# Decode's convolution rows on another DMA queue, and single instructions held at their traced place, in a two-layer Conformer and RWKV-7 step

## The chip, the core and the metric

The kernel runs on one core of a Trainium2 chip, in one launch. The metric is the device time of one execution in microseconds (us), the lower the better. The engines are named as the profile names them: PE (TensorE matmuls) with its weight loads PEld, DVE (VectorE), ACT (ScalarE), POOL (GpSimd) and SP (SyncE, which here only issues DMAs). Every engine works off its own list of instructions in order, and waits where an instruction needs a result that is not there yet.

## What is computed

One inference step of a decoder of two layers in float32, for a prompt of 1,024 rows (16 learned rows are put ahead of it) and for 8 decode rows. Layer 0 mixes tokens by a causal convolution module, layer 1 by RWKV-7 time mixing. Each is followed by a squared-ReLU MLP.

```python
D_MODEL, SEQ, DEC_BATCH, N_META, CONV_WIDTH, D_FF = 1024, 1024, 8, 16, 31, 4096

# layer 0
u = h @ w_pw1 + b_pw1
u = u[..., :D_MODEL] * sigmoid(u[..., D_MODEL:])
full = concatenate([buf, u], axis=1)                 # buf: the last 30 rows of u, state_conv
c = depthwise_conv(full, w_dw, width=31) + b_dw
out = silu(layernorm(c)) @ w_pw2 + b_pw2             # new state: full[:, -30:]

# layer 1
xx = prev - h                                        # prev: h of the row before
r, k, v = (h + xx * x_mix[i]) @ w_r, ... @ w_k, ... @ w_v
decay = exp(-exp(-softplus(-(w0 + tanh(xw @ w1) @ w2)) - 0.5))
a, g = sigmoid(a0 + (xa @ a1) @ a2), sigmoid(xg @ g1) @ g2
S = S * w + (S @ -kk) (kk * a)^T + v k^T             # for every row, 16 heads of 64
y = S @ r
out = ((groupnorm(y) + bonus) * g) @ w_o

# both
h = h + out
h = h + square(relu(rmsnorm(h) @ w_in)) @ w_out
```

One of the outputs, conv_sample, is the convolution state of the 8 decode rows: for each, 29 of its old 30 rows moved up by one and a new row behind them. The 29 old rows are copied from DRAM to DRAM by a DMA and touch no engine's memory.

## The kernel before, in words

**Work and tiles.** The 1,040 prompt rows and the 8 decode rows stand as columns, the 1,024 features as 8 blocks of 128 partitions. A float32 product is made of three matmuls: a weight block is split into hi (a cast on ACT, `L156`) and lo (a subtraction on POOL in four quarters, `L161`), an activation likewise (`L139` on ACT, `L140` on DVE), and PE adds hi by hi, hi by lo and lo by hi (`L186` to `L188`).

**Layer 0** goes over three groups of columns (352, 348, 348). At the start, group 0 is loaded (`xt0_*`) and transposed, its first weight blocks `pg0_*` and `pa0_*` are loaded and split, and PE makes `ps_g0_*` and `ps_a0_*`; the input of group 1 (`xt1_*`) is loaded and transposed into `tx1_*` in between. The convolution runs on DVE, the second product and the MLP follow. The start function (around `L690`) issues the eight copies of conv_sample on POOL's own DMA queue (`L696`), and there POOL's and ACT's instructions keep the order of the program.

**Layer 1** makes its mixer in four groups g of 272, 256, 256 and 264 columns: `prepare(g)` loads `hx` (`L863`), makes the differences `xx` (`L867`; blocks k = 2 and 5 on POOL, the other six on DVE) and the mixed inputs `mx{g}_{i}_{k}` (`L874`); PE makes `pk`, `pr`, `pv` of each pair of heads (`L900`). Each chunk c of 64 rows also needs the inverse of small triangular blocks: `inverses` loads `ni{c}` (`L1184`), runs a chain of some 60 short DVE instructions (`L1192`, `L1193`), stores it, and `front` loads it again as `p32` (`L1220`), transposes it into `x32` on DVE (`L1223`) and uses it on PE as `gg` (`L1280`). `norm_gate` normalises the result (`ey`, `eq`, `ems`, `L1452` to `L1459`), adds `ebv` (`L1476`), multiplies by the gate `egt` (`L1477`) and stores `d_z`.

**The output product.** `mixer_out(g)` runs for three column groups (328, 352, 352). It loads the residual `h1_g` (`L1572`), the gated result `zr` (`L1580`) and the weight blocks `wo{g}_{m}` (`L145`), splits `zr` into `z_h` and `z_l`, makes `ps_oo{g}_{m}` and adds it to `h1_g` on DVE (`L1590`); ACT squares the sum into `sq{g}_{m}` (`L248`). Then comes the MLP of layer 1.

**What sets the order.** A list scheduler of the framework sees the whole program and orders each engine's instructions by its own estimate of when their inputs are there. Inside `tc.manual_schedule(engines=...)` the named engines keep the order of the program. `tc.keep_in_program_order(x)` does so for one instruction: it may not go ahead of the instruction that was written before it on the same engine; others can still move.

Of the kernel before, what the change touches and what calls it, by code (L numbers as in the profile page):

```python
# [8 lines left out]
F32 = mybir.dt.float32  # L9
# [7 lines left out]
P = 128  # L17
# [29 lines left out]
def hybrid_step(tc, x_prompt, x_sample, state_conv, state_shift, state_wkv, meta_tokens,  # L47
# [10 lines left out]
    with ctx:  # L58
# [72 lines left out]
        def open_weights(stack, raw_bufs, bufs, tag):  # L131
# [3 lines left out]
            cur["bufs"] = bufs  # L135

        def split(hi, lo, src, eng_lo):

            nc.scalar.copy(hi, src)  # L139
            eng_lo.tensor_sub(lo, src, hi.bitcast(F32))  # L140
# [6 lines left out]

        def load_w(src, shape, name, eng_lo, tag="w", raw=None):

            a, b = shape  # L150
            if raw is None:
                raw = load_raw(src, shape, name)
            nb = cur["bufs"][tag]
            hi = cur["wsp"].tile([P, 8 * P], F32R, name=f"{name}_hi", tag=tag + "h", bufs=nb)
            lo = cur["wsp"].tile([P, 8 * P], F32R, name=f"{name}_lo", tag=tag + "l", bufs=nb)
            nc.scalar.copy(hi[:, :a * b], raw[:, :a * b])  # L156

            step = 2 * P if eng_lo is nc.gpsimd else a * b
            for c in range(0, a * b, step):
                cs = slice(c, min(c + step, a * b))  # L160
                eng_lo.tensor_sub(lo[:, cs], raw[:, cs], hi[:, cs].bitcast(F32))  # L161
            v = lambda t: t[:, :a * b].rearrange("p (a b) -> p a b", a=a)
            return v(hi), v(lo)

        def col_src(w, m):

            return w[:, m * P:(m + 1) * P].rearrange("(k p) c -> p k c", p=P)

        def load_col(w, m, name, eng_lo, tag="w"):
            return load_w(col_src(w, m), (KT, P), name, eng_lo, tag)  # L170

# [216 lines left out]
        with ExitStack() as l0:  # L388
# [158 lines left out]
            def conv_dec(c, c_col):  # L547
# [5 lines left out]
                for m in range(KT):  # L553
# [6 lines left out]
                    nc.gpsimd.tensor_copy(win[:, :, CB:CW], udec[:, m, :].unsqueeze(2))  # L560
                    nc.vector.tensor_mul(win, win, wdw[:, m:m + 1, :].broadcast_to([P, DEC, CW]))
                    rd = decp.tile([P, DEC], F32, name=f"rd{m}", tag="rd")
                    nc.vector.tensor_reduce(rd, win, axis=AX.X, op=ALU.add)
# [118 lines left out]
            with ExitStack() as s:  # L682
# [8 lines left out]
                first = pw1_weights(0, 0)  # L691

                def between():
                    ready.append(next(first))
                    for q in range(DEC):
                        nc.gpsimd.dma_start(o_conv_sample[0, q, 0:CB - 1, :], state_conv[0, q, 1:CB, :])  # L696
                with tc.manual_schedule(engines={nc.scalar.engine, nc.gpsimd.engine}):
                    for _ in transpose_x(0, *acts[0], between):
                        pass
                    ready.append(next(first))  # L700
# [151 lines left out]
        def prepare(g):  # L852
# [13 lines left out]
            for k in range(KT):  # L866
                (nc.gpsimd if k % 3 == 2 else nc.vector).tensor_sub(xx[:, k, :npr], hx[:, k, 0:npr], hx[:, k, 1:1 + npr])  # L867
                yield
# [66 lines left out]
        def mixer_in(g, tick):  # L935
# [86 lines left out]
            def finish(p, rk, ab, vv):  # L1022
                def trace():
# [20 lines left out]

                    n32 = pr.tile([P, 5, 32], F32, name=nm("n32", p), tag="n32", bufs=2)
                    if g == 0:
# [131 lines left out]
        def inverses(c, n):  # L1178
# [5 lines left out]
            nc.sync.dma_start(ni, blocks(d_n))  # L1184
            yield 5
            top = META if c == 0 else 32
            aside = bank(f"tt{c}", "x")[:B] if c + n == NCH else None
            for j in range(top - 2, 0, -1):
                wd = top - 1 - j
                o = aside if aside is not None else wk.tile([P, 256], F32, name=f"tt{c}_{j}", tag="tt")[:B]  # L1190
                o = o[:, :j * wd].rearrange("p (s t) -> p s t", t=wd)
                nc.vector.tensor_mul(o, ni[:, :j, j:j + 1].broadcast_to([B, j, wd]), ni[:, j:j + 1, j + 1:top].broadcast_to([B, j, wd]))  # L1192
                nc.vector.tensor_add(ni[:, :j, j + 1:top], ni[:, :j, j + 1:top], o)  # L1193
                if j % 4 == 0:
                    yield 1.5
# [13 lines left out]
        def front(c):  # L1209
# [12 lines left out]
            x32 = w_([P, KT, 32], "x32", c)  # L1222
            nc.vector.transpose(flat(x32), flat(p32))  # L1223
            mask = lambda x: m_ar[:, x].unsqueeze(1).broadcast_to([P, 4, HS])
# [216 lines left out]
        def norm_gate():  # L1441
# [20 lines left out]
            def load_rest(hf, lo, n):  # L1462

                two = [w_([P, KH * P], tag, f"{lo}_{hf}") for tag in ("ebv", "egt")]
                for t, src in zip(two, (d_bv, d_g)):
# [3 lines left out]
            def gated(pt, hf, lo, n, bv, gt):  # L1469
# [5 lines left out]
                w = KH * n  # L1475
                nc.vector.tensor_add(bv[:, :w], z[:, :w], bv[:, :w])  # L1476
                nc.vector.tensor_mul(gt[:, :w], bv[:, :w], gt[:, :w])  # L1477
# [80 lines left out]
        with ExitStack() as l1:  # L1558
# [10 lines left out]
            def mixer_out(g, residp, actp, fill, add):  # L1569
                lo, n = G2[g]  # L1570
                h1 = hl[g] = residp.tile([P, KT, cur["wide"]], F32, name=f"h1_{g}", tag="h")
                nc.sync.dma_start(h1[:, :, :n], d_h[:, :, lo:lo + n])  # L1572
                block = lambda m: load_col(rwkv_w_o[0], m, f"wo{g}_{m}", nc.gpsimd)
                z = new_acts(actp, f"z{g}", cur["wide"])
# [100 lines left out]
            add, sums = sums_of(1)  # L1675
            mixer_out(1, residp2, actp, lambda: None, add)
            g1 = group(1, actp, hidp, sums)
            fill, rest = filler(2 * KT + MLP2_POINTS, ([ranked(FN, final(0))], FB))
            add, sums = sums_of(2)
            mixer_out(2, residp2, actp2, fill, add)  # L1680
            end = []
# [41 lines left out]
```

## Time and profile before

| what | before |
|---|---|
| time, median of 3 runs (lowest, highest) | 2708.15 us (2705.03, 2711.84) |
| the profiled execution | 2712.1 us |
| its span, first to last instruction | 2710.4 us |
| granted TensorE clock, mean over the span | 0.982 |
| PE busy | 2618.3 us, 97% |
| DVE busy | 1724.8 us, 64% |
| POOL busy | 1450.1 us, 54% |
| ACT busy | 1138.6 us, 42% |
| HBM traffic over the span | 147 GB/s |

In the profile's timelines a row gives the start in us, the busy time, the engine (SPq, POOLq and ACTq are those engines' DMA issues), line and operation, the tiles without their numbers, the form, and in brackets how long the engine had idled before it and what released it. In the tables by stretch of time, each engine has its busy us and in parentheses its instructions; then come the granted clock of PE (1.00 is full), the busy share of the 16 DMA engines and GB/s.

### The profile page before, as it was taken

What the parts mean: (1) busy time and instruction counts of PE and PEld (TensorE: products, weight loads), DVE (VectorE), ACT (ScalarE), POOL (GpSimd) and SP (SyncE); (2) the same over time, 40 slices, a digit from 0 to 9 for tenths busy, and PEclk for the clock granted to TensorE, in tenths of its full rate; (3) what the DMA queues carried; (4) which work ended last, traced back from release to release, by engine and by line L of the source; (5) the groups of instructions that cost most, each with busy time, mean ns of one, the idle gap of its engine ahead of it and who ended that gap; (6) DMA issues with size and microseconds to landing.
All of it is one profiled execution on the core that took longest, in us unless ns stands there. A gap on an engine that the chain in (4) does not pass through costs nothing.

```text
span 2710.4 us, 51412 instructions
## 1 busy us (share of the span) xinstructions
PE 2618.3 (97%) x19796; PEld 2462.4 (91%) x19796; DVE 1724.8 (64%) x3584; ACT 1138.6 (42%) x2101; POOL 1450.1 (54%) x2068
## 2 busy tenths in 40 slices
PE   8999999999999999998999998979999899999998
PEld 7999999999999999777787886769999899999998
DVE  5999999997445345345767576676679643334435
ACT  5546435444444333333344544544444542222223
POOL 6677878877878775022111112366678753333331
PEclk9999999999999999999999998989999899999999
DMA  6653544554456442668768867786655632222211
GB/s 184 170 165 113 163 139 125 157 179 133 139 157 195 135 138 86 203 190 207 196 167 208 197 168 188 186 202 166 155 162 176 199 110 75 70 71 67 66 55 43
DMA packets 602058, 400.20 MB, mean 148 GB/s; under 512 B 96128, under 2 KB 548928, under 8 KB 601814
## 3 DMA queue, kind: packets, MB, share of 16 engines
q1 hardware_dynamic: 539716, 350.74, 46.4%
q10 hardware_dynamic: 53122, 18.88, 3.3%
q0 software_dynamic: 8976, 27.30, 3.1%
q8 instruction: 156, 2.56, 0.4%
q14 instruction: 88, 0.72, 0.1%
HBM read 338.94 MB, written 58.83 MB: 147 GB/s over the span
## 4 chain that ended last, share of the span: by engine, by line
PE 80%; DVE 10%; DMA 4%; issue 2%; ACT 2%; POOL 2%; ACTq 0%; SPq 0%; DVEq 0%; POOLq 0%
PE ps_in L186 8%; PE ps_in L187 8%; PE ps_in L188 8%; PE out L186 8%; PE out L187 8%; PE out L188 8%; PE pk L900 4%; PE pr L900 3%; PE pv L900 3%; PE ps_o L186 1%; PE ps_o L188 1%; PE ps_o L187 1%; PE ps_a L187 1%; PE ps_a L188 1%; PE ps_g L186 1%
## 5 line engine op out<-in xcount | busy, mean ns | idle before, releaser
L161 POOL TENSOR_TENSOR wo_lo<-wo_raw,wo_hi 128x256 fp32r<-128x256 f32 x736 | 540.2, 766 | 293.8 <-ACT wo_hi L156 289.8
L161 POOL TENSOR_TENSOR wi_lo<-wi_raw,wi_hi 128x256 fp32r<-128x256 f32 x640 | 471.3, 768 | 258.8 <-ACT wi_hi L156 250.2
L186 PE MATMUL out<-hh,wo_hi 128*128 128x352 f32 (+2 forms) x1536 | 500.0, 326 | 14.3 <-DVE hl L140 7.7
L188 PE MATMUL ps_in<-m_l,wi_hi 128*128 128x352 f32 (+2 forms) x1536 | 493.6, 321 | 3.6 <-DVE m_l L284 3.6
L353 DVE TENSOR_TENSOR h<-h,out 128x352 f32<-128x352 f32 (+2 forms) x768 | 387.4, 513 | 172.2 <-PE out L188 170.7
L186 PE MATMUL ps_in<-m_h,wi_hi 128*128 128x352 f32 (+2 forms) x1536 | 494.9, 322 | 0.7 <-ACT m_h L283 0.7
L187 PE MATMUL out<-hh,wo_lo 128*128 128x352 f32 (+2 forms) x1536 | 494.7, 322 | 0.0
L188 PE MATMUL out<-hl,wo_hi 128*128 128x352 f32 (+2 forms) x1536 | 493.5, 322 | 0.0
L187 PE MATMUL ps_in<-m_h,wi_lo 128*128 128x352 f32 (+2 forms) x1536 | 492.7, 321 | 0.0
L534 DVE SCALAR_TENSOR_TENSOR cv<-u,wdw,cv 128x352 f32<-128x352 f32 (+2 forms) x720 | 379.3, 578 | 0.6
L156 ACT CAST wi_hi<-wi_raw 128x1024 fp32r<-128x1024 f32 x160 | 167.9, 1049 | 410.5 <-PE out L188 197.7
L156 ACT CAST wo_hi<-wo_raw 128x1024 fp32r<-128x1024 f32 x184 | 192.9, 1048 | 346.0 <-PE out L188 163.6
L186 PEld LDWEIGHTS out<-hh,wo_hi 128*128 128x128 f32 x1536 | 291.3, 190 | 19.9 <-DVE hl L140 9.2
L188 PEld LDWEIGHTS ps_in<-m_l,wi_hi 128*128 128x128 f32 x1536 | 289.0, 188 | 5.7 <-DVE m_l L284 4.6
L186 PEld LDWEIGHTS ps_in<-m_h,wi_hi 128*128 128x128 f32 x1536 | 289.8, 189 | 2.9 <-ACT m_h L283 1.2
L187 PEld LDWEIGHTS out<-hh,wo_lo 128*128 128x128 f32 x1536 | 290.9, 189 | 0.8
L188 PEld LDWEIGHTS out<-hl,wo_hi 128*128 128x128 f32 x1536 | 290.0, 189 | 0.0
L187 PEld LDWEIGHTS ps_in<-m_h,wi_lo 128*128 128x128 f32 x1536 | 289.1, 188 | 0.9
L341 DVE SCALAR_TENSOR_TENSOR ps_in<-ps_in,rs_m 128x352 f32<-128x352 f32 (+2 forms) x192 | 100.5, 525 | 247.0 <-PE ps_in L188 246.6
L140 DVE TENSOR_TENSOR hl<-ps_in,hh 128x352 fp32r<-128x352 f32 (+2 forms) x192 | 98.8, 516 | 125.4 <-ACT hh L139 125.1
L342 ACT ACTIVATE ps_in<-ps_in 128x352 f32<-128x352 f32 (+2 forms) x192 | 84.9, 443 | 121.3 <-DVE ps_in L341 121.0
L900 PE MATMUL pv<-mx,wv_raw 128*128 128x256 f32 (+2 forms) x512 | 131.3, 401 | 1.2 <-ACT rk L1080 1.2
(368 smaller groups left out, 4687.9 us busy)
## 6 DMA issues: line engine op xcount, KB each, us to landing
wi_raw<-in_w_mlp_in_dram SPq DMA_DIRECT2D x160, 512.0 KB, 4.1
wo_raw<-in_w_mlp_out_dram SPq DMA_DIRECT2D x160, 512.0 KB, 3.7
wk_raw<-in_rwkv_w_k_dram SPq DMA_DIRECT2D x32, 512.0 KB, 8.3
wr_raw<-in_rwkv_w_r_dram SPq DMA_DIRECT2D x32, 512.0 KB, 5.8
wv_raw<-in_rwkv_w_v_dram SPq DMA_DIRECT2D x32, 512.0 KB
d_ab<-ab POOLq DMA_DIRECT2D x32, 512.0 KB, 4.7
pg_raw<-in_conv_w_pw_dram SPq DMA_DIRECT2D x24, 512.0 KB, 12.8
pa_raw<-in_conv_w_pw_dram SPq DMA_DIRECT2D x24, 512.0 KB, 4.1
```

The source lines that it names most:

```text
L140: eng_lo.tensor_sub(lo, src, hi.bitcast(F32))
L156: nc.scalar.copy(hi[:, :a * b], raw[:, :a * b])
L161: eng_lo.tensor_sub(lo[:, cs], raw[:, cs], hi[:, cs].bitcast(F32))
L186: nc.tensor.matmul(ps, w[0], act[0], start=first, stop=False)
L187: nc.tensor.matmul(ps, w[1], act[0], start=False, stop=False)
L188: nc.tensor.matmul(ps, w[0], act[1], start=False, stop=last)
L341: nc.vector.scalar_tensor_tensor(s, s, 0.0, rs()[:, :n], op0=ALU.max, op1=ALU.mult)
L342: nc.scalar.activation(s, s, AF.Square)
L353: nc.vector.tensor_add(hv[:, 4 * i + m, :], hv[:, 4 * i + m, :], ps[:, :n])
L534: nc.vector.scalar_tensor_tensor(acc[m][:, :n], ug[:, m, j:j + n], wdw[:, m, j:j + 1], acc[m][:, :n], op0=ALU.mult, op1=ALU.add)
L900: nc.tensor.matmul(ps[:, :n], w[:, k, :], act[k], start=k == 0, stop=k == KT - 1)
```

## The change

No arithmetic is added or taken away. Eight DMAs change their queue and place, eight kinds of instruction are held to the one written before them, two calls keep PE's program order, and three buffer counts change:

1. The eight copies of conv_sample leave the start (POOL's queue) and are issued by SP in `conv_dec`, one for each of its eight steps, each held behind the SP load written before it. The start's fixed order is now for ACT alone.
2. The hi casts of the blocks `wo{g}_1` to `wo{g}_7` on ACT are held.
3. For g = 1 to 3 the difference `xx` of k = 0 (DVE) and of k = 2 (POOL) is held.
4. The first multiplication of every chain of `inverses`, every `x32` transpose and every `ebv` addition on DVE are held; `inverses` yields once more ahead of its chain.
5. `n32` has one buffer for two, `ebv` one, `egt` two.
6. `mixer_out(1)` and `mixer_out(2)` run in `in_order()`, so PE keeps the program's order there.

```diff
+        kept_place = tc.keep_in_program_order
...
-            nc.scalar.copy(hi[:, :a * b], raw[:, :a * b])
+            cast = nc.scalar.copy(hi[:, :a * b], raw[:, :a * b])
+            if keep:
+                kept_place(cast)
...
                     nc.vector.tensor_mul(win, win, wdw[:, m:m + 1, :].broadcast_to([P, DEC, CW]))
+                    kept_place(nc.sync.dma_start(o_conv_sample[0, m, 0:CB - 1, :], state_conv[0, m, 1:CB, :]))
...
-                def between():
-                    ready.append(next(first))
-                    for q in range(DEC):
-                        nc.gpsimd.dma_start(o_conv_sample[0, q, 0:CB - 1, :], state_conv[0, q, 1:CB, :])
-                with tc.manual_schedule(engines={nc.scalar.engine, nc.gpsimd.engine}):
-                    for _ in transpose_x(0, *acts[0], between):
+                with tc.manual_schedule(engines={nc.scalar.engine}):
+                    for _ in transpose_x(0, *acts[0], lambda: ready.append(next(first))):
...
             for k in range(KT):
-                (nc.gpsimd if k % 3 == 2 else nc.vector).tensor_sub(xx[:, k, :npr], hx[:, k, 0:npr], hx[:, k, 1:1 + npr])
+                first = (nc.gpsimd if k % 3 == 2 else nc.vector).tensor_sub(xx[:, k, :npr], hx[:, k, 0:npr], hx[:, k, 1:1 + npr])
+                if g and k in (0, 2):
+                    kept_place(first)
...
-                    n32 = pr.tile([P, 5, 32], F32, name=nm("n32", p), tag="n32", bufs=2)
+                    n32 = pr.tile([P, 5, 32], F32, name=nm("n32", p), tag="n32")
...
             yield 5
+            yield 1
...
-                nc.vector.tensor_mul(o, ni[:, :j, j:j + 1].broadcast_to([B, j, wd]), ni[:, j:j + 1, j + 1:top].broadcast_to([B, j, wd]))
+                first = nc.vector.tensor_mul(o, ni[:, :j, j:j + 1].broadcast_to([B, j, wd]), ni[:, j:j + 1, j + 1:top].broadcast_to([B, j, wd]))
+                if j == top - 2:
+                    kept_place(first)
...
-            nc.vector.transpose(flat(x32), flat(p32))
+            kept_place(nc.vector.transpose(flat(x32), flat(p32)))
...
-                two = [w_([P, KH * P], tag, f"{lo}_{hf}") for tag in ("ebv", "egt")]
+                two = [w_([P, KH * P], tag, f"{lo}_{hf}", bufs=b) for tag, b in (("ebv", 1), ("egt", 2))]
...
-                nc.vector.tensor_add(bv[:, :w], z[:, :w], bv[:, :w])
+                kept_place(nc.vector.tensor_add(bv[:, :w], z[:, :w], bv[:, :w]))
...
-                block = lambda m: load_col(rwkv_w_o[0], m, f"wo{g}_{m}", nc.gpsimd)
+                block = lambda m: load_col(rwkv_w_o[0], m, f"wo{g}_{m}", nc.gpsimd, keep=m > 0)
...
-            mixer_out(1, residp2, actp, lambda: None, add)
+            with in_order():
+                mixer_out(1, residp2, actp, lambda: None, add)
...
-            mixer_out(2, residp2, actp2, fill, add)
+            with in_order():
+                mixer_out(2, residp2, actp2, fill, add)
```

What this does to the lists of the engines is seen at four places. On PE at the start, before, behind the first matmuls of group 0 (`ps_g0_*`, `ps_a0_*`) stand the three transposes of the first feature block of group 1, `tx1_0`, each from one of the loads `xt1_0` to `xt1_2`:

```order
L186 MATMUL ps_a0_0_354<-hn0_h_133,pa0_0_hi_286 128x352
L188 MATMUL ps_g0_0_306<-hn0_l_134,pg0_0_hi_217 128x352
L186 MATMUL ps_g0_1_399<-hn0_h_133,pg0_1_hi_383 128x352
L186 MATMUL ps_a0_1_426<-hn0_h_133,pa0_1_hi_392 128x352
L475 MATMUL tx1_0_439<-ident_58,xt1_0_319 128x128
L475 MATMUL tx1_0_439<-ident_58,xt1_1_326 128x128
L475 MATMUL tx1_0_439<-ident_58,xt1_2_333 128x92
L187 MATMUL ps_a0_0_354<-hn0_h_133,pa0_0_lo_287 128x352
```

On PE at the start, after, first the end of the stretch with the two transposes, then where the third one stands, 46 rows further on:

```order
L191 MATMUL ps_a0_0_346<-hn0_h_133,pa0_0_lo_279 128x352
L192 MATMUL ps_a0_0_346<-hn0_l_134,pa0_0_hi_278 128x352
L190 MATMUL ps_a0_0_346<-hn0_h_133,pa0_0_hi_278 128x352
L190 MATMUL ps_a0_1_418<-hn0_h_133,pa0_1_hi_384 128x352
L479 MATMUL tx1_0_431<-ident_58,xt1_0_311 128x128
L479 MATMUL tx1_0_431<-ident_58,xt1_1_318 128x128
...
L191 MATMUL ps_a0_1_418<-hn0_h_133,pa0_1_lo_385 128x352
L192 MATMUL ps_a0_1_418<-hn0_l_134,pa0_1_hi_384 128x352
L479 MATMUL tx1_0_431<-ident_58,xt1_2_325 128x92
```

The transposes of group 1 moved behind matmuls of group 0 that need none of its loads; the third stands behind all of `ps_a0_0` and `ps_g0_1`.

On DVE at the third group of the mixer (`xx3`, `mx3_2_*`; `tt5`, `ni5` are the chain of chunk 5), before:

```order
L1193 TENSOR_TENSOR ni5_15485<-ni5_15485,tt5_19_15654 128x19x12
L867 TENSOR_TENSOR xx3_15791<-hx3_15740 128x256 x3
L870 TENSOR_TENSOR xx3_15791<-sps_12349,hx3_15740 128x8x8
L1134 SCALAR_TENSOR_TENSOR rk2_0_15735<-rk22_0_15585,pvec_85,wa2_0_15611 128x256
L867 TENSOR_TENSOR xx3_15791<-hx3_15740 128x256 x3
L1192 TENSOR_TENSOR tt5_18_15657<-ni5_15485 128x234
L1476 TENSOR_TENSOR ebv16_1_15579<-ez16_1_15643,ebv16_1_15579 128x512
L874 SCALAR_TENSOR_TENSOR mx3_2_0_15801<-xx3_15791,pvec_85,hx3_15740 128x264
```

On DVE there, after:

```order
L867 TENSOR_TENSOR xx3_15779<-hx3_15677 128x256 x2
L872 TENSOR_TENSOR xx3_15779<-sps_12349,hx3_15677 128x8x8
L867 TENSOR_TENSOR xx3_15779<-hx3_15677 128x256 x3
L1195 TENSOR_TENSOR tt5_18_15682<-ni5_15481 128x234
...
L1195 TENSOR_TENSOR tt5_8_15772<-ni5_15481 128x184
L1198 TENSOR_TENSOR ni5_15481<-ni5_15481,tt5_8_15772 128x8x23
L867 TENSOR_TENSOR xx3_15779<-hx3_15677 128x256
L1195 TENSOR_TENSOR tt5_7_15826<-ni5_15481 128x168
L876 SCALAR_TENSOR_TENSOR mx3_2_0_15789<-xx3_15779,pvec_85,hx3_15677 128x264
L876 SCALAR_TENSOR_TENSOR mx3_2_1_15791<-xx3_15779,pvec_85,hx3_15677 128x264
```

Five of DVE's six differences stay; the held one and with it `mx3_2_*` moved from the chain's step 18 to behind its step 8.

On ACT ahead of the output product of group 0, before:

```order
L156 CAST wo0_0_hi_19691<-wo0_0_raw_19689 128x1024
L1038 COPY vt3_6_19368<-vt3_6_19367 128x256
L1039 DMA d_v_76<-vt3_6_19368 128x2x128
L156 CAST wo0_1_hi_19720<-wo0_1_raw_19718 128x1024
L1263 DMA sv_12350<-d_v_76 64x8x64 x2
...
L1457 ACTIVATE ems11_19498<-ems11_19498,eps_t_65 128x8
L156 CAST wo0_3_hi_19817<-wo0_3_raw_19815 128x1024
L156 CAST wo0_4_hi_19854<-wo0_4_raw_19852 128x1024
L139 CAST z0_h0_19671<-zr00_19687 128x328
L139 CAST z0_h1_19672<-zr00_19687 128x328
```

On ACT there, after:

```order
L1462 ACTIVATE ems11_19498<-ems11_19498,eps_t_65 128x8
L1041 DMA d_v_76<-vt3_7_19546 128x2x128
L141 CAST z0_h0_19671<-zr00_19687 128x328
L141 CAST z0_h1_19672<-zr00_19687 128x328
...
L141 CAST z0_h7_19678<-zr06_19712 128x328
L158 CAST wo0_1_hi_19720<-wo0_1_raw_19718 128x1024
L158 CAST wo0_2_hi_19729<-wo0_2_raw_19727 128x1024
```

The casts of `z0` moved ahead of those of `wo0_1` to `wo0_4`.

On ACT at the output product of group 1 (`sq1_0` squares the first finished block of `h1_1`; `ez1040` is decode's), before:

```order
L224 ACTIVATE sq_f02_24465<-h1_0_19669 128x328
L156 CAST wo1_3_hi_24104<-wo1_3_raw_24102 128x1024
...
L1474 ACTIVATE ez1040_1_23983<-ynd_1_23978,pvec_85 128x8 x4
L156 CAST wo1_7_hi_24257<-wo1_7_raw_24255 128x1024
...
L248 ACTIVATE sq1_0_24100<-h1_1_24005 128x352
L248 ACTIVATE sq1_1_24137<-h1_1_24005 128x352
```

On ACT there, after:

```order
L1479 ACTIVATE ez1040_1_23983<-ynd_1_23978,pvec_85 128x8 x4
L252 ACTIVATE sq1_0_24102<-h1_1_24007 128x352
L158 CAST wo1_3_hi_24106<-wo1_3_raw_24104 128x1024
L252 ACTIVATE sq1_1_24139<-h1_1_24007 128x352
L158 CAST wo1_4_hi_24143<-wo1_4_raw_24141 128x1024
```

The cast of `wo1_3` moved behind `sq1_0`, and each later one behind the square of the next block.

More of the change, by code (lines that the diff above doesn't have):

```diff
@@ L146, in load_raw, with load_w @@
             return raw
-        def load_w(src, shape, name, eng_lo, tag="w", raw=None):
+        def load_w(src, shape, name, eng_lo, tag="w", raw=None, keep=False):
             a, b = shape
@@ L167, in col_src, with load_col @@
             return w[:, m * P:(m + 1) * P].rearrange("(k p) c -> p k c", p=P)
-        def load_col(w, m, name, eng_lo, tag="w"):
-            return load_w(col_src(w, m), (KT, P), name, eng_lo, tag)
+        def load_col(w, m, name, eng_lo, tag="w", keep=False):
+            return load_w(col_src(w, m), (KT, P), name, eng_lo, tag, keep=keep)
         def blocks_of(raw):
```

## The prediction

> **What bounds the kernel now.** I read the page first: shares of the span, then the chain that ended last.
>
> ```profile
> PE 2618.3 (97%) x19796; PEld 2462.4 (91%) x19796; DVE 1724.8 (64%) x3584; ACT 1138.6 (42%) x2101; POOL 1450.1 (54%) x2068
> ...
> PE 80%; DVE 10%; DMA 4%; issue 2%; ACT 2%; POOL 2%; ACTq 0%; SPq 0%; DVEq 0%; POOLq 0%
> ```
>
> PE works 97% of the span. So nothing that the change does to another engine counts unless it closes or opens a hole on PE, and the holes are few. The windows by stage show where there is none and where there is one (columns: busy time of PE, its weight loads, DVE, ACT, POOL with counts, then the granted clock, the DMA share, GB/s).
>
> ```profile
> 32.00:36.00 4.00, 3.61 (x14) 3.55 (x15) 0.45 (x2) 3.13 (x6) 1.13 (x2) 0.50 0.63 180
> 36.00:40.00 4.00, 4.00 (x24) 4.00 (x23) 1.59 (x5) 3.55 (x7) 2.99 (x5) 0.87 0.82 235
> 40.00:220.00 180.00, 180.00 (x1169) 178.73 (x1168) 169.32 (x350) 86.75 (x137) 128.43 (x197) 1.00 0.56 158
> 550.00:725.00 175.00, 175.00 (x1087) 172.71 (x1087) 130.87 (x258) 84.16 (x128) 140.65 (x193) 1.00 0.50 151
> ```
>
> From 40 to 220 us and from 550 to 725 us PE is busy for all 180.00 and 175.00 us. A hole closed before such a stretch is therefore kept to its end, and work put beside it is free as long as PE is fed. The timeline of PE, filtered for idle time (in brackets: idle before, and what ended it), gives the holes that the change touches.
>
> ```profile
> 26.28 0.33 PE L475 MATMUL tx<-ident,xt 128*128 128x128 f32 x1 [0.66 <-DMA xt<-in_x_prompt_dram]
> 28.10 0.33 PE L475 MATMUL tx<-ident,xt 128*128 128x128 f32 x1 [1.50 <-DMA xt<-in_x_prompt_dram]
> 32.39 0.42 PE L475 MATMUL tx<-ident,xt 92*128 92x92 f32 x1 [3.96 <-DMA xt<-in_x_prompt_dram]
> ...
> 1285.35 1.22 PE L1099 MATMUL l_a<-lwa,wa 64*128 64x256 f32 x2 [5.60 <-DVE rk L1112]
> ...
> 1458.47 0.46 PE L1053 MATMUL nn<-ab 64*32 64x32 f32 x32 [2.22 <-DVE ab L1144]
> 1460.88 0.58 PE L798 MATMUL pb<-r16h,hspread 128*128 128x256 f32 x1 [1.32 <-ACT vv L1105]
> 1461.47 3.98 PE L900 MATMUL pk<-mx,wk_raw 128*128 128x264 f32 x12
> ...
> 1475.38 0.63 PE L1298 MATMUL bT<-ident,bk 128*128 128x128 f32 x4 [1.40 <-DVE nr L1239]
> 1476.64 0.63 PE L1298 MATMUL bT<-ident,bk 128*128 128x128 f32 x4 [0.63 <-DVE nr L1239]
> ...
> 1645.73 0.59 PE L798 MATMUL pb<-r16h,hspread 128*128 128x264 f32 x1 [4.80 <-ACT vv L1105]
> ...
> 1781.94 0.64 PE L186 MATMUL ps_oo<-z_h,wo_hi 128*128 128x328 f32 x1 [11.06 <-ACT z_h L139]
> ...
> 2144.07 0.66 PE L186 MATMUL ps_oo<-z_h,wo_hi 128*128 128x352 f32 x1 [5.15 <-DVE h L1590]
> ```
>
> The sum is made against the profiled execution (2712.1 us, span 2710.4); a term moves both alike, so I apply it to the median of the three runs, 2708.15.
>
> **The start, −8.4 us (bounds −4 to −9).** PE waits three times for the loads of `xt1`, 0.66 + 1.50 + 3.96 = 6.12 us, and then runs at half clock: 3.61 us at 0.50 lose 1.8 and 4.00 at 0.87 lose 0.5, together 2.3. In the new order the first matmuls of group 0 stand ahead of these transposes, and POOL's copies of the convolution rows are gone from in front of the loads.
>
> ```profile
> 11.36 2.78 POOL L161 TENSOR_TENSOR pg_lo<-pg_raw,pg_hi 128x256 fp32r<-128x256 f32 x4 [7.43 <-ACT pg_hi L156]
> 14.08 3.90 POOL L696 DMA_DIRECT2D out_dram<-in_state_conv_dram  x8
> ```
>
> PE can now starve on weights only: POOL makes one block's low half in 2.78 us, and the block's 24 matmuls need 24 × 0.154 = 3.7 us (180.00 / 1169 from the window). The supply is faster, so the holes close. The low bound keeps about half of the idle time, for the loads of the second block's weights, which stand behind more of `xt` traffic.
>
> **The copies on SP, 0 (bounds 0 to +12).** Eight copies of 116 KB are issued between weight loads, amid a stage where PE is full. What hides them is slack in the weight supply. The lines of ACT in that window say what its casts waited for:
>
> ```profile
> L156 ACT CAST wi_hi<-wi_raw 128x1024 fp32r<-128x1024 f32 x23 | 24.1, 1049 | 48.3 <-PE ps_in L188 23.6 <-PE out L188 20.1 <-POOL wo_lo L161 3.0
> ```
>
> Never for a DMA; so a load that lands 1 or 2 us later costs nothing. The other end: each copy, read and written (0.232 MB) at the window's 151 GB/s, holds the rings 1.5 us, and eight with no cover 12 us.
>
> **`xx2`, −0.8 us.** The hole of 5.60 us at 1285.35 ends on DVE's `rk`, and just ahead of that stand
>
> ```profile
> 1283.10 1.41 DVE L867 TENSOR_TENSOR xx<-hx 128x256 f32<-128x256 f32 x4
> 1284.44 0.47 DVE L874 SCALAR_TENSOR_TENSOR mx<-xx,pvec,hx 128x256 f32<-128x256 f32 x1
> ```
>
> One subtraction (1.41 / 4 = 0.35) and one `mx` (0.47) now come behind `rk`: 0.8. The same pin in the second group (`xx1`) moves an `mx` behind four `ab` products, work of about the same length on both sides: 0, ±1.
>
> **`xx3`, +5.8 us (bounds 0 to +12).** One subtraction of `xx3` is held behind the chain's step `tt5_8`, and `mx3_2` with it, which feeds `pk3_0`, PE's 12 matmuls at 1461.47. In the trace of before that step, of the 184-wide product, is at 1474.00:
>
> ```profile
> 1451.38 2.07 DVE L874 SCALAR_TENSOR_TENSOR mx<-xx,pvec,hx 128x264 f32<-128x264 f32 x5
> ...
> 1474.00 0.34 DVE L1192 TENSOR_TENSOR tt<-ni 128x184 f32<-128x184 f32 x1
> ...
> 1451.38:1474.34 22.96, 22.61 (x53) 0.93 0.71 176
> ```
>
> DVE is full between (22.61 of 22.96 us, mean 0.43). From it leave eight `mx` (8 × 0.41 = 3.3), which now come later, some ten others that did run before `tt5_8` and now run behind (the second group's `xa` and `nr`, `fs`, `sv`, `ems`, `rk2_0`: 10 × 0.43 = 4.3), and an estimated 1.5 of slowing; some 1.0 comes in. DVE reaches `mx3_2_0` at 1474.34 − 9.1 + 1.0 = 1466.2, and with the product and the handover `pk3_0` can start at 1467.0, not 1461.47: +5.5. PE is there early, since what waits 2.22 and 1.32 now stands elsewhere, so it idles about 10 us and pays the half clock again (2.3, as at the start); in return the holes of 1.40 and 0.63 at 1475 go, filled by then. 5.5 + 2.3 − 2.0 = 5.8. The lower end is a wait that never comes, rival B; the upper end is DVE reaching `tt5_8` no sooner than before (1474.3 + 0.8 − 1461.5 = 13.6, less 2.0).
>
> **The stall at 1645, −2.3 us (bounds 0 to −4.8).** Ahead of it ACT switches its table twice:
>
> ```profile
> 1638.75 1.28 ACT L1457 ACT_TABLE_LOAD   x1
> ...
> 1642.08 1.28 ACT L1115 ACT_TABLE_LOAD   x1
> ```
>
> The square roots behind one switch now come after the exponentials, so about both 1.28 us, less 0.3, leave the path to `vv`. The rest of the 4.80 stays.
>
> **The output product of group 0, −6 us (bounds −3 to −9).** PE waits 11.06 us for the casts of `z0`. ACT's timeline there:
>
> ```profile
> 1761.80 1.04 ACT L156 CAST wo_hi<-wo_raw 128x1024 fp32r<-128x1024 f32 x1 [6.23 <-DMA wo_raw<-in_rwkv_w_o_dram]
> ...
> 1772.15 0.30 ACT L1457 ACTIVATE ems<-ems,eps_t 128x8 f32<-128x8 f32 x1
> ...
> 1780.48 1.04 ACT L156 CAST wo_hi<-wo_raw 128x1024 fp32r<-128x1024 f32 x1 [5.87 <-DMA wo_raw<-in_rwkv_w_o_dram]
> 1781.43 3.03 ACT L139 CAST z_h<-zr 128x328 fp32r<-128x328 f32 x8
> ```
>
> The casts of `z0` stand behind casts of weights that wait 6.23 and 5.87 us for their loads. In the new order they stand right behind the `ems` of 1772.15: up to 1781.43 − 1772.45 = 9.0 earlier. They then wait for the last of `d_z`, and DVE's next chain becomes the limit, which in before starts only at
>
> ```profile
> 1785.87 0.20 DVE L1192 TENSOR_TENSOR tt<-ni 128x30 f32<-128x30 f32 x1
> ```
>
> 4.4 us behind the casts of `z0`, with loads on SP that do not move forward as far. I take two thirds of 9.
>
> **The output product of group 1, +2.8 us (bounds −1 to +6).** The cast of `wo1_3`, done early before, is now behind the square of `h1_1`'s first block, and so behind
>
> ```profile
> 2135.36 5.08 SPq L1572 DMA_DIRECT2D h<-d_h  x2
> ...
> 2143.50 1.82 DVE L1590 TENSOR_TENSOR h<-h,ps_oo 128x352 f32<-128x352 f32 x4 [2.55 <-DMA h<-d_h]
> ```
>
> I estimate that load to land at 2140.3, 3.2 us sooner, since one earlier issue on SP leaves its place (1.7 us) and the two issues, which took 5.08 us together, close up by 1.5. Then 0.45 for the add, 0.45 for the square, 1.05 for the cast and 0.7 for the first low half: the third block starts at 2143.0, takes 3.84, and the fourth begins at 2146.9 less the 1.07 that the clock after a shorter hole gives back, against 2144.07: +2.8.
>
> Sum: −8.4 − 0.8 + 5.8 − 2.3 − 6.0 + 2.8 = −8.9, so 2708.15 − 8.9 = 2699.
>
> **The rivals.**
> B, the wait at `pk3_0` does not come: DVE gets to `tt5_8` before PE wants `pk3_0`, because `hx3` arrives sooner. Then the holes of 2.22, 1.32, 1.40 and 0.63 go too (−5.6): −8.4 − 0.8 − 5.6 − 2.3 − 6.0 + 2.8 = −20.3, 2688; 2682 if the output product gives all 9 and more. For it: the bound of 0 above. Against: DVE's full 22.61.
> C, the output product gives nothing, since the later weights or DVE's chain hold PE as long: −2.9, 2705. For it: the 4.4 us between `z0` and the chain.
> D, slower: the pins of the chains' first product and of the transpose of `p`. In before DVE fills waits with the next group's work; pinned, the instruction's place is fixed behind such work, or all behind it waits for its load. What is lost at most per chunk is the work now between, such as
>
> ```profile
> 1296.53 0.27 DVE L1055 TENSOR_TENSOR n<-nn,nmask 128x128 f32<-128x128 f32 x1
> ...
> 1298.90 0.68 DVE L1144 TENSOR_TENSOR ab<-wa,em 128x512 f32<-128x512 f32 x1
> ...
> 1661.87 0.45 DVE L1223 STREAM_TRANSPOSE x<-p 128x256 f32<-128x256 f32 x1 [1.82 <-DMA p<-d_p]
> ```
>
> about 2.5 us from `n` to `ab`. At three quarters of it, 1.9, on 12 chunks: +22.5, 2722. It decides from 0.75 us per chunk for no gain, from 1.4 (17.1 / 12) for slower. For it: DVE has no slack where it waits 1.82 us for `p`. Against: the transposes stand directly before their use.
> E, the copies hold the weight loads behind them on SP's queue: +12, 2711. Against: casts that never waited for a DMA. [...]
>
> **How the numbers follow.** A measurement of this kernel tells about 0.3%, 8.1 us, from no change: faster is below 2700.0, slower above 2716.3. My forecast has 0.40 (own range 2692 to 2706: 0.23 faster, 0.16 same, 0.01 slower), B 0.21 (faster), C 0.08 (same), D 0.26 (slower), E 0.05 (same). Sum: faster 0.44, same 0.29, slower 0.27. The range reaches from B's far end, 2682, to D, 2722; half of D lies above, and a little of B below.
>
> **What would show it.** At the start: no idle time on PE for `xt`, clock 1.00 by 32 us. From 550 to 725: PE 175 of 175 still. At `pk3_0`: a wait of some 10 us that ends on DVE's `mx`, or none (B). At 1645: a shorter wait on `vv`. At the output product: `z_h` cast right behind `ems`. At group 1: the third block waits for `wo_lo`. Idle time of PE between 1285 and 1645 that grows by more than 1.4 us a chunk, ended by DVE's `ab` or `rk`, makes D true and the forecast wrong.

## The result and the profile after

The changed kernel takes 2712.47 us (median of 20 runs, 2705.15 to 2720.22), the kernel before 2706.66 (median of 20, 2702.11 to 2711.84): 5.8 us more, ratio 1.002 (95% interval 1.0012 to 1.0027). The forecast was 2699, a gain of 9. The time lies within the stated range, but the sign was wrong. (The three runs the forecast started from have a median of 2708.15, 1.5 above that of the 20.) The profiled execution of the changed kernel took 2716.26 us with a span of 2714.5. Single runs of one kernel lie up to 8 us to each side of their median, so the two profiles are compared stage by stage, not by their spans.

At the start the prediction's reading holds. The windows (PE, weight loads, DVE, ACT, POOL, clock, DMA share, GB/s) of the changed kernel, with the stage in which SyncE now issues the eight copies as the last row:

```profile
28.00:32.00 4.00, 3.89 (x25) 3.61 (x24) 0.00 (x0) 3.94 (x7) 4.00 (x7) 1.00 0.91 185
32.00:36.00 4.00, 4.00 (x27) 4.00 (x26) 3.89 (x2) 3.67 (x8) 4.00 (x7) 1.00 0.88 228
36.00:40.00 4.00, 4.00 (x28) 3.98 (x27) 3.96 (x7) 3.97 (x7) 3.36 (x7) 1.00 0.95 251
...
319.00:471.00 152.00, 149.50 (x933) 148.09 (x932) 146.22 (x304) 73.46 (x119) 122.98 (x170) 1.00 0.46 138
```

PE works through at clock 1.00 where it had idled and then run at 0.50 and 0.87. For the copies, the same 152 us of the kernel before, 7 us later on the clock, are

```profile
326.00:478.00 152.00, 149.94 (x935) 148.43 (x934) 145.83 (x303) 73.41 (x120) 123.10 (x170) 1.00 0.45 132
```

and differ by two matmul records and 0.4 us of PE's busy time. The copies stand at 319 to 471 us, in an earlier stage than the 550 to 725 that the prediction looked at. What hides them, a weight supply with slack, is the same there, for the casts of that stretch wait for no DMA either:

```profile
L158 ACT CAST wi_hi<-wi_raw 128x1024 fp32r<-128x1024 f32 x20 | 21.0, 1050 | 45.5 <-PE out L192 22.8 <-PE ps_in L192 21.1 <-issue 1.7
```

At `pk3_0` PE's timeline has the wait that was forecast as some 10 us, in two pieces, 3.50 + 6.17 = 9.7; at 1645 the stall of 4.80 is down to 2.57:

```profile
1457.85 0.39 PE L798 MATMUL pb<-r16h,hspread 128*128 128x256 f32 x1 [3.50 <-DVE n L1057]
...
1464.53 0.78 PE L902 MATMUL pk<-mx,wk_raw 128*128 128x264 f32 x1 [6.17 <-issue]
...
1651.57 0.39 PE L798 MATMUL pb<-r16h,hspread 128*128 128x264 f32 x1 [2.57 <-ACT vv L1107]
```

The first piece ends on DVE's `n`. For the second the profile names no releaser ("issue"), but DVE's order does: the held difference and the first `mx3_2` (0.48 us, to 1464.42) end just before the matmul starts.

```profile
1463.36 0.42 DVE L867 TENSOR_TENSOR xx<-hx 128x256 f32<-128x256 f32 x1
1463.70 0.33 DVE L1195 TENSOR_TENSOR tt<-ni 128x168 f32<-128x168 f32 x1
1463.94 3.31 DVE L876 SCALAR_TENSOR_TENSOR mx<-xx,pvec,hx 128x264 f32<-128x264 f32 x8
```

At the output product of group 0 the first wait did shrink, from 11.06 to 2.26. A second one came behind it, and 50 us later a third:

```profile
1769.78 0.64 PE L190 MATMUL ps_oo<-z_h,wo_hi 128*128 128x328 f32 x1 [2.26 <-ACT z_h L141]
...
1777.92 0.64 PE L192 MATMUL ps_oo<-z_l,wo_hi 128*128 128x328 f32 x1 [4.30 <-DVE z_l L142]
...
1829.14 0.64 PE L192 MATMUL ps_in<-m_l,wi_hi 128*128 128x328 f32 x1 [7.69 <-DVE m_l L288]
```

The matmul at 1829.14 needs `m_l`, the low half of the next stage's input, which DVE makes. The timelines of DVE and of POOL, cut to what ran just then:

```profile
1820.24 8.85 DVE L288 SCALAR_TENSOR_TENSOR m_l<-h,pvec,m_h 128x328 fp32r<-128x328 f32 x1
```

```profile
1820.52 5.49 POOL L165 TENSOR_TENSOR wi_lo<-wi_raw,wi_hi 128x256 fp32r<-128x256 f32 x8
1825.97 2.75 POOL L165 TENSOR_TENSOR wo_lo<-wo_raw,wo_hi 128x256 fp32r<-128x256 f32 x4
```

One instruction of DVE, which takes 0.55 us in the kernel before at 1825.13, lasts 8.85: as long as POOL runs its twelve instructions without a gap, and 0.36 beyond. PE's matmuls, counted in their order, show what that costs: from the 12000th to the 13200th (1686 to 1788 us in before) the changed kernel gains 7.7 us on the kernel before, and by the 13800th (1854 us) 7.0 of them are lost again. In the kernel before the same group of rows holds a small one of these: 2.89 us beside a run that ends after four (2.79 us), and PE waits 2.01:

```profile
1825.13 0.55 DVE L284 SCALAR_TENSOR_TENSOR m_l<-h,pvec,m_h 128x328 fp32r<-128x328 f32 x1
...
1826.21 2.89 DVE L284 SCALAR_TENSOR_TENSOR m_l<-h,pvec,m_h 128x328 fp32r<-128x328 f32 x1 [0.53 <-ACT m_h L283]
```

```profile
1825.95 2.79 POOL L161 TENSOR_TENSOR wi_lo<-wi_raw,wi_hi 128x256 fp32r<-128x256 f32 x4
```

At the output product of group 1 PE waits 7.29 us instead of 5.15, and then again in the last block, where nothing waited before:

```profile
2141.95 0.66 PE L190 MATMUL ps_oo<-z_h,wo_hi 128*128 128x352 f32 x1 [7.29 <-ACT wo_hi L158]
...
2176.36 0.43 PE L191 MATMUL ps_oo<-z_h,wo_lo 128*128 128x352 f32 x1 [0.33 <-POOL wo_lo L165]
...
2183.63 0.42 PE L190 MATMUL ps_oo<-z_h,wo_hi 128*128 128x352 f32 x1 [0.98 <-ACT wo_hi L158]
2184.44 0.43 PE L191 MATMUL ps_oo<-z_h,wo_lo 128*128 128x352 f32 x1 [0.38 <-POOL wo_lo L165]
```

### The profile page after: what moved, and what is told of

Read it like the earlier page. It is cut to its first block, busy times and chain, and to the rows that moved or that the text cites. A ratio compares the mean times of both kernels' runs of the same rounds, so it can differ in the third digit from the quotient of the medians.

```text
span 2714.5 us, 51394 instructions
## 1 busy us (share of the span) xinstructions
PE 2614.7 (96%) x19796; PEld 2458.5 (91%) x19796; DVE 1734.2 (64%) x3584; ACT 1137.6 (42%) x2101; POOL 1444.7 (53%) x2060
## 5 line engine op out<-in xcount | busy, mean ns | idle before, releaser
L538 DVE SCALAR_TENSOR_TENSOR cv<-u,wdw,cv 128x348 f32<-128x348 f32 (+2 forms) x720 | 377.3, 572 | 0.7
L902 PE MATMUL pk<-mx,wk_raw 128*128 128x256 f32 (+2 forms) x512 | 125.6, 395 | 7.5 <-issue 6.2
```

Of the source, the lines that this page charges most:

```text
L538: nc.vector.scalar_tensor_tensor(acc[m][:, :n], ug[:, m, j:j + n], wdw[:, m, j:j + 1], acc[m][:, :n], op0=ALU.mult, op1=ALU.add)
L902: nc.tensor.matmul(ps[:, :n], w[:, k, :], act[k], start=k == 0, stop=k == KT - 1)
```

## The experiments

Theory from the profile after: the start gains as forecast; the pins on `xx` lose as forecast or more; the kept casts lose, since their gain at group 0 is taken back while POOL holds up DVE's `m_l`. The rival for the last: DVE is simply late there. Every kernel below was timed beside the kernel before, with 10 to 12 runs each, the last two with 5. The parts change PE's order in separate places: the start among the first 3,410 matmuls, the chains between the 7,780th and the 12,980th, the casts between the 16,220th and the 16,710th; the pins on `xx` swap one pair. The two scopes around `mixer_out` have no run of their own, so it is not shown that they do nothing: in the output product of group 1 PE's order in the changed kernel is not that of the kept casts alone.

**The start alone.** The lines of the diff with `o_conv_sample` and with `manual_schedule(engines={nc.scalar.engine})`, on the kernel before:

```
-  nc.gpsimd.dma_start(o_conv_sample[0, q, ...], state_conv[0, q, ...])   (between)
+  kept_place(nc.sync.dma_start(o_conv_sample[0, m, ...], state_conv[0, m, ...]))   (conv_dec)
```

> The kernel before with the start part alone: the convolution rows copied by SyncE amid the pointwise stages, GpSimd scheduled freely at the start. Theory (the prediction's first term): PE's three waits for the loads of group 1 (0.66 + 1.50 + 3.96 us) and the half clock behind them (2.3 us) go, the copies are hidden, 8 us less than before; PE busy 175 of 175 us in the stage with the copies. Rival (the copies hold weight loads on SyncE's queue): PE loses 5 to 12 us there and the sum is 0 to -3. What the trace of after shows is 8.5 us gained at the start, of which 1.5 us had been lost on the first loads.

2700.18 us against 2706.37: −6.2, ratio 0.9976 (0.9967 to 0.9985). In its trace the 300th matmul starts 6.9 us earlier than in before's, and the 5100th (830 us in before) 5.9. Rival E, which wanted 5 to 12 us lost between them, falls: the copies cost 1 us at most.

**The pins on `xx` alone.**

```
+                if g and k in (0, 2):
+                    kept_place(first)
```

> The kernel before with the pins on the differences of the mixer (xx1 to xx3) alone. Theory of the prediction: -0.8 us at 1285 and +5.8 us at pk3_0, where PE waits some 10 us for DVE: +5 in all. Here the held difference of the third group stands still later in DVE's list (behind the chain's step 4, not 8), so the wait may be longer. Rival: the later stretches, where PE waits for the same DVE work anyway, give it back, and the whole is within 2 us of before.

2715.24 us against 2706.37: +8.9, ratio 1.0029 (1.0018 to 1.0039), more than forecast. PE's timeline has the wait at `pk3_0`, 10.59 us, and one in the first group, 2.19 at 1159.16 where before has 1.22 at 1157.51:

```profile
1159.16 0.50 PE L1073 MATMUL pk<-rk,hsum 128*128 128x272 f32 x1 [2.19 <-ACT vv L1109]
...
1470.43 0.78 PE L904 MATMUL pk<-mx,wk_raw 128*128 128x264 f32 x1 [10.59 <-issue]
```

```profile
1157.51 0.50 PE L1069 MATMUL pk<-rk,hsum 128*128 128x272 f32 x1 [1.22 <-ACT vv L1105]
```

**The pins on `xx` in groups 1 and 2 only.**

```
-                if g and k in (0, 2):
+                if g in (1, 2) and k in (0, 2):
```

> The kernel before with the pins on the differences of the mixer in groups 1 and 2 alone, not in group 3. Theory: what p_xx loses (+9 us in time, +9.95 at pk3_0 in its trace) is the pin of the third group; without it 0 to -1 us against before. Rival: the loss comes from all three groups, +3 to +6 us.

2708.83 us against 2705.12: +3.7, ratio 1.0012 (1.0003 to 1.0020). So the third group's pin costs 8.9 − 3.7 = 5.2, near the forecast 5.8. The first two, which I had put at −0.8 and 0, lose some 3.7, with an interval of 0.8 to 5.4. The trace shows one place for it, the wait for `vv` at 1160.50, now 1.94 (the first row):

```profile
1160.50 0.66 PE L1073 MATMUL pk<-rk,hsum 128*128 128x272 f32 x1 [1.94 <-ACT vv L1109]
...
1289.17 0.79 PE L1103 MATMUL l_a<-lwa,wa 64*128 64x256 f32 x1 [4.66 <-DVE rk L1116]
```

That wait is 0.7 longer, and in the trace with all `xx` pins 1.0. In all nine kernels without these pins it is 1.21 or 1.22, in the changed kernel 2.10. It costs more than its own length: from the 6940th to the 7000th matmul the two kernels take 2.4 and 2.5 us more than the one with the start alone. The wait at 1285, which the pin of the second group was to shorten, does get shorter: from 5.60 to 4.66 here (the second row, at 1289.17), 4.77 with all pins and 4.85 in the changed kernel, against 5.15 to 5.86 in the kernels without pins. What is left of the 3.7 is not placed. So the 0 to −1 expected of this run did not come, and its time is in the rival's +3 to +6; but by the trace it is the first group that loses, not the second.

**The chain part alone.** Pins on `tt`, `x32` and `ebv`, `n32` with one buffer less, `egt` with one more, one more `yield`. (`ebv` has one buffer in both kernels; the number is only written out. So two buffer counts change, not three, and the expectation below has `ebv` wrong.)

```
+                if j == top - 2:
+                    kept_place(first)
...
+            kept_place(nc.vector.transpose(flat(x32), flat(p32)))
```

> The kernel before with the chain part alone: the chain's first product, the transpose of p and decode's addition hold their place, n32 and ebv have one buffer less, one more step between load and chain. Theory of the prediction: 0 to -2 us (1285 and pk3_0 as before, the wait of 4.80 us at 1645 shorter by 2.3). Rival D: the pinned instructions hold DVE, many short waits of PE between 1285 and 1645 for ab, rk or vv, +4 to +20 us.

2707.17 us against 2706.37: +0.8, ratio 1.0002 (0.9993 to 1.0011), no change. Both theories are half right. From the 9900th to the 11400th matmul (1497 to 1627 us in before) this kernel loses 5.0 us that the kernels without the chain part do not lose: rival D in small. From there to the 12000th (1686 us) it wins back some 4.6 more than they do, with the shorter stall at 1645 and with the small waits at 1681 and 1682 that are gone.

**The kept casts alone.**

```
-  nc.scalar.copy(hi[:, :a * b], raw[:, :a * b])
+  cast = nc.scalar.copy(hi[:, :a * b], raw[:, :a * b])
+  if keep:
+      kept_place(cast)
```

> The kernel before with the kept place of the casts of the output product's weights alone. Theory of the prediction: at the output product of group 0 the wait of 11.06 us falls by 6 and the gain stays, at group 1 +2.8: -3 us in all. Theory from the trace of after: the casts of z0 come 9 us sooner, but the weights of the next stage are then cast in one run, GpSimd works without a pause, and one m_l on DVE is held for as long as GpSimd goes on (8.85 us in after): the 9 us are given back; at group 1 +2.5 and another +2.6 where the last weight's cast comes late: +4 to +6 in all.

2711.21 us against 2706.37: +4.8, ratio 1.0018 (1.0009 to 1.0027). DVE's `m_l` lasts 8.85 us again, beside a run of twelve, which is the second theory:

```profile
1815.70 8.85 DVE L288 SCALAR_TENSOR_TENSOR m_l<-h,pvec,m_h 128x328 fp32r<-128x328 f32 x1
```

From the 12000th to the 13200th matmul (1686 to 1788 us in before) it gains 11.8 us on the kernel before, and by the 13800th (1854 us) 10.7 of them are lost again; from the 16200th to the 16800th, the output product of group 1, it loses 5.6 more. In the five traces where the casts are not kept (before, the start alone, the two with pins on `xx`, the chain part alone) no `m_l` there lasts longer than 2.89.

**The changed kernel without the pins on `xx`.**

> The changed kernel without the pins on the differences of the mixer. If the parts add up: 2706.4 - 6.2 + 0.8 + 4.8 = 2706, 6 to 7 us less than the changed kernel, no wait of 6 us at pk3_0. Rival (DVE's chains cost as much in the changed order): within 2 us of the changed kernel, 2711 to 2714.

2707.33 us against 2705.12: +2.2, ratio 1.0004 (0.9995 to 1.0013), some 3.6 less than the changed kernel's +5.8: less than the 6 to 7 expected, more than the 2 of the rival. The wait of 6 us at `pk3_0` is gone; the longest on a `pk` there is 0.88. Here POOL's run beside the `m_l` has eight instructions, and `m_l` lasts 6.13:

```profile
1809.23 6.13 DVE L288 SCALAR_TENSOR_TENSOR m_l<-h,pvec,m_h 128x328 fp32r<-128x328 f32 x1
```

```profile
1809.51 2.77 POOL L165 TENSOR_TENSOR wi_lo<-wi_raw,wi_hi 128x256 fp32r<-128x256 f32 x4
1812.25 2.75 POOL L165 TENSOR_TENSOR wo_lo<-wo_raw,wo_hi 128x256 fp32r<-128x256 f32 x4
```

**Two low halves moved from POOL to DVE, beside the kept casts.**

```
-  return load_col(w_in, j, f"wi{layer}_{groups[0][0]}_{j}", eng_w)
+  return load_col(w_in, j, f"wi{layer}_{groups[0][0]}_{j}",
+                  nc.vector if layer and not groups[0][0] and j in (2, 3) else eng_w)
```

> The kernel before with the kept place of the casts (as p_keep) and, beside it, the low halves of two weight blocks, the third and fourth of the stage behind the output product of group 0, made by DVE in one instruction each, and no longer by GpSimd in eight. Theory (DVE's m_l is held as long as GpSimd's run of instructions lasts): the run shrinks from 12 instructions to 4 or has a hole, no m_l lasts longer than 3 us, of the 9 us that p_keep lost again some 5 to 7 stay gained; against p_keep -4 to -6 us. Rival (m_l waits for something else, or DVE is simply behind): m_l of 8 to 9 us as in p_keep, and the two instructions more on DVE (some 1.1 us each) make it 0 to +2 us against p_keep.

2708.11 us against 2705.12: +3.0, ratio 1.0008 (0.9999 to 1.0017); against the kept casts alone about −1.8, which the intervals do not separate, and less than the 4 to 6 expected. The trace shows the step: POOL's run has four instructions, the longest `m_l` lasts 3.41. From the 12000th to the 13800th matmul this kernel gains 4.6 us on the kernel before, the kept casts alone 1.1. PE waits 4.53 for the first `m_l` here, so part of the rival stands too: DVE, with two instructions more, is late.

**The start and the kept casts of group 0 only.** `keep=not g and m > 0`, all low halves on POOL.

> The start part and the kept place of the casts in group 0 alone; all low halves on GpSimd as in before. It tells what the two low halves on DVE do in best1, and what group 1's kept casts cost in p_keep. Theory: m_l held for a run of 12 instructions (8.85 us) as in p_keep, the group-0 gain lost, 2706 - 6.2 - 0.5 = 2699, some 3 to 4 us above best1, no wait for wo_hi at group 1. Rival (best1's gain is group 1 without its kept casts, not the low halves): 2695 to 2697 as best1.

2701.35 us against 2706.30: −5.0, ratio 0.9979 (0.9970 to 0.9987), no better than the start alone (−6.2), as its theory has it, and group 1 has no wait for `wo_hi`. The `m_l` lasts 8.86:

```profile
1814.50 8.86 DVE L288 SCALAR_TENSOR_TENSOR m_l<-h,pvec,m_h 128x328 fp32r<-128x328 f32 x1
```

**The same with two low halves on DVE.**

> A version that takes what seemed to pay: the start part, the kept place of the casts in group 0 alone (group 1 as in before), and the two low halves on DVE as in k_dve; no pins on differences or chains. If GpSimd's run is what took the gain back: -6 at the start and -5 to -8 at the output product, 2692 to 2696. If it is not: -6 alone, 2699 to 2702.

2696.10 us against 2705.12: −9.0, ratio 0.9965 (0.9953 to 0.9977), at the edge of what was expected. `m_l` and POOL's run:

```profile
1809.15 3.41 DVE L288 SCALAR_TENSOR_TENSOR m_l<-h,pvec,m_h 128x328 fp32r<-128x328 f32 x1
```

```profile
1809.42 2.77 POOL L165 TENSOR_TENSOR wo_lo<-wo_raw,wo_hi 128x256 fp32r<-128x256 f32 x4
```

**And with two more**, the low halves of the first two blocks of the second matrix:

```
-  yield load_w(src, (2, 4 * P), f"wo{layer}_{groups[0][0]}_{b}_{i}", eng_w)
+  yield load_w(src, (2, 4 * P), f"wo{layer}_{groups[0][0]}_{b}_{i}",
+               nc.vector if layer and not groups[0][0] and b == 0 else eng_w)
```

> best1 with the low halves of the first two blocks of the second weight matrix on DVE as well, so that GpSimd has hardly anything beside the m_l. Theory (m_l is held as long as GpSimd's run lasts): no m_l above 1.5 us, PE's waits of 4.53 and 2.15 us for m_l in best1 shrink by 2 to 3, 2693 to 2695. Rival (DVE itself is the bound there, each low half some 1.1 us on it): same as best1 or up to 2 us above.

2692.34 us against 2706.30: −14.0, ratio 0.9942 (0.9928 to 0.9956), the fastest of all. POOL has no run left there but the two instructions and a DMA issue below, and the `m_l` behind them take 0.5 us each:

```profile
1810.99 2.84 POOL L165 TENSOR_TENSOR wi_lo<-wi_raw,wi_hi 128x256 fp32r<-128x256 f32 x2
1813.78 0.59 POOL L1197 DMA_DIRECT2D d_p<-ni  x1
```

```profile
1814.59 1.02 DVE L288 SCALAR_TENSOR_TENSOR m_l<-h,pvec,m_h 128x328 fp32r<-128x328 f32 x2
...
1815.93 1.49 DVE L288 SCALAR_TENSOR_TENSOR m_l<-h,pvec,m_h 128x328 fp32r<-128x328 f32 x3
```

PE's wait of 4.53 for the first `m_l` is still there, so not all expectations held: two low halves, 1.21 and 1.27 us on DVE, stand ahead of that `m_l`. The gain came from the second wait, 2.15 in the version before, now gone. From the 12000th to the 13800th matmul the two traces differ by 3.9 us; the rest of the 5 us between the two medians is not placed.

The same stretch compares the last three kernels. Up to the 13200th matmul they gain 12.0, 12.0 and 12.6 us on the kernel before; from there to the 13800th they lose 13.3, 8.3 and 5.0, with runs of twelve, four and no POOL instructions beside the `m_l`. By this the run accounts for some 8 of the 13, and 5 are lost without it.

## Why the prediction was wrong

- **The start, −8.4.** Measured −6.2 (−4.1 to −8.9 by the interval). Right in kind, inside the bounds of −4 to −9. **The copies, 0:** right, for the reason given; the stage was the wrong one. That the weight loads stand behind the copies, for 12 us in all, as the upper bound and rival E have it, no run shows: with the start alone the eight copies cost 1 us at most (6.9 less 5.9).
- **`xx3`, +5.8.** Right: a wait of 9.7 us where some 10 were forecast, and 8.9 − 3.7 = 5.2 by the two runs. In their traces the stretch from the 9000th to the 9900th matmul (1406 to 1497 us) differs by 4.7.
- **`xx2`, −0.8.** By the traces right: the wait at 1285 fell from 5.60 to between 4.66 and 4.85. **`xx1`, 0 ± 1.** Failed: the two together measure +3.7 (0.8 to 5.4). "Work of about the same length on both sides" was wrong for `xx1`. The wait for `vv` in the first group grew from 1.22 to 1.94, 2.10 and 2.19 in the three kernels with the pin. That the moved `mx` delay what `vv` needs is argued from the order and was not tried by itself.
- **The stall at 1645, −2.3.** It fell from 4.80 to 2.57, 2.2, but only half for the reason given. Of the two table loads one is gone; the other, for the square root, still stands just ahead of `vv`:

```profile
1649.56 1.28 ACT L1462 ACT_TABLE_LOAD   x1
1650.86 0.30 ACT L1462 ACTIVATE ems<-ems,eps_t 128x8 f32<-128x8 f32 x1
1651.06 0.18 ACT L1126 COPY wc<-ex 128x4 f32<-128x4 f32 x1
1651.15 0.37 ACT L1107 COPY vv<-pv 128x264 f32<-128x264 f32 x1
```

One load is 1.28, so that the number fits to 0.1 is luck. And the chain part as a whole is +0.8: rival D takes some 5 us between 1497 and 1627, about what the stall and its neighbours give back.
- **The output product of group 0, −6.** This is the step that failed. At the output product itself it holds: the hole of 11.06 went to 2.26, a new one of 4.30 came for `z_l`, and the stretch up to the 13200th matmul gains 7.7. But the prediction looked for what comes next on DVE's chain alone and put the stage behind at nothing. There POOL's run of low halves is longer once the casts are kept (eight to twelve instructions in a row beside that `m_l`, against four), and it holds one `m_l` for 8.85 us; 7.0 of the 7.7 are lost. With the kept casts of group 0 beside the start the gain is −5.0 + 6.2 = +1.2; with four low halves taken off POOL as well it is −14.0 + 6.2 = −7.8 (each with some 3 to 4 us to either side). So a gain like the 6 us could be kept, and the collision with POOL's run took most of it. No run moves the low halves without keeping the casts; the kernel before also waits 3.6 us for `m_l`, so a part of the −7.8 may be had without them.
- **The output product of group 1, +2.8.** Mis-sized: 5.6 with the kept casts alone, 4.6 in the changed kernel. The prediction's own figures give less than it wrote: 2146.9 less 1.07 is 1.8 behind 2144.07, not 2.8, which would have made the sum −9.9. In the changed kernel the first wait grew by 2.1. What the term left out is that a cast held behind a square delays the last block too (0.33, 0.98 and 0.38 us of waits for `wo_hi` and `wo_lo`).

The four parts alone sum to −6.2 + 8.9 + 0.8 + 4.8 = +8.3, the change measures +5.8; each carries an interval of some 2.5 us to either side, so the parts add up as far as can be told. Against the prediction's −8.9 the sum of parts is 17.2 higher. Of that, 8.0 lie in the kept casts (+4.8 for −3.2: group 0 and group 1 together), 4.5 in `xx1` and `xx2`, 3.1 in the chain with its stall (+0.8 for −2.3), 2.2 in the start, less 0.6 for `xx3`. The kept casts alone would have brought the forecast to no change; it took the others to make it slower.

That POOL's run holds DVE is shown by length, in seven kernels: runs of 12, 12, 12, 8, 4, 4 and 0 instructions go with an `m_l` of 8.85, 8.85, 8.86, 6.13, 3.41, 3.41 and 0.55 us. Other `m_l` beside POOL take turns with it, near 1 us each (2.92 / 3 = 0.97, POOL's two 1.94 / 2 = 0.97), as these do in the changed kernel just before the long one:

```profile
1817.39 2.92 DVE L288 SCALAR_TENSOR_TENSOR m_l<-h,pvec,m_h 128x328 fp32r<-128x328 f32 x3
```

```profile
1818.02 1.94 POOL L165 TENSOR_TENSOR wi_lo<-wi_raw,wi_hi 128x256 fp32r<-128x256 f32 x2
```

Why the long one doesn't stays open. In the changed kernel (1820.24, issue from 1819.90 to 1820.49), without the pins on `xx` (1809.23, 1808.90 to 1809.49) and in the kernel of the −9.0 (1809.15, 1808.81 to 1809.40) it starts during one of POOL's DMA issues, which makes the issue a suspect. But the issue alone does not do it. In the fastest kernel an `m_l` starts during the same issue (at 1814.11, the issue runs from 1813.78 to 1814.37), no run follows, and it takes 0.55. Nor is it needed: in the changed kernel an `m_l` at 522.27 is held for 3.14 us with no issue near, and it ends 0.38 us behind the POOL instruction at 524.07, although POOL goes on.

```profile
522.27 3.14 DVE L288 SCALAR_TENSOR_TENSOR m_l<-h,pvec,m_h 128x348 fp32r<-128x348 f32 x1
```

```profile
521.28 2.83 POOL L165 TENSOR_TENSOR p_lo<-p_raw,p_hi 128x256 fp32r<-128x256 f32 x4
524.07 0.96 POOL L263 TENSOR_TENSOR u<-u 128x352 f32<-128x352 f32 x1
524.98 1.03 POOL L165 TENSOR_TENSOR p_lo<-p_raw,p_hi 128x256 fp32r<-128x256 f32 x1
```

What couples the two engines is not shown. The trace has the lengths: the `m_l` of 8.85 us, which reads `h` and `m_h`, was held by twelve POOL instructions in a row, not by one of 0.7, and it ends 0.36 us behind the last of them.

## What to carry to other kernels

A cast or a load that is freed to come earlier also frees what it feeds. Follow it to the engine that works on it next, and ask what that engine's longer run will sit beside, one stage further on. Here DVE's `m_l` and POOL's low halves took turns at near 1 us each (0.97), or one `m_l` was shut out for POOL's whole run (8.85 us); a single instruction many times as long as others of the same shape (8.85 against 0.55) was the sign of it in the timeline. The cure was to take work off the engine that ran through (in the fastest kernel no run is left and the `m_l` takes 0.55), and its price was that the other engine got later (two low halves of 1.21 and 1.27 us stand ahead of the first `m_l`, for which PE waits 4.53).

## What the runs showed of the hardware

- DVE's `m_l`, which reads `h` and `m_h` and took 0.55 us at 1825.13 in the kernel before, was held for 8.85 us beside an unbroken run of twelve POOL instructions of 0.7 us. The length repeats in three kernels, 8.85, 8.85 and 8.86.
- It is not `m_l` alone: at 32.27 us of the changed kernel DVE's `dg`, 0.47 us at 38.77, lasted 5.41 beside eight POOL subtractions. PE was busy all the time there (4.00 of 4.00 us in both windows), so PE lost nothing by it there.
- PE's clock in the 8 us of that wait is 0.50, and the wait is paid twice: first as idle time, then as half speed in the matmuls behind it, 0.27 us from one to the next (1831.28 to 1831.55) at 0.50 against 0.15 (1836.04 to 1836.19) at 1.00 (PE, weight loads, DVE, ACT, POOL, clock; the second row is the next 4 us, with PE busy for 3.86 at 0.50, the third the clock back at 1.00):

```profile
1821.00:1829.00 8.00, 0.45 (x2) 0.04 (x1) 8.00 (x1) 0.00 (x0) 7.73 (x12) 0.50 0.89 244
1829.00:1833.00 4.00, 3.86 (x14) 3.75 (x15) 2.38 (x6) 0.94 (x2) 0.00 (x0) 0.50 0.76 232
...
1836.00:1840.00 4.00, 4.00 (x29) 4.00 (x28) 3.49 (x6) 0.81 (x2) 1.22 (x2) 1.00 0.32 85
```
